# A two-layer decoder trunk on one core: two blocks of the expert product U h taken ahead of the second norm

## The chip, the core and the metric

The kernel runs on one core of one Trainium2 chip. The metric is the device time of one execution in microseconds (us). Five engines work from queues of their own and wait for one another through semaphores: TensorE (PE, matrix products), VectorE (DVE), ScalarE (ACT), GpSimd (POOL) and SyncE (SP, which here only issues transfers). ACT issues transfers too, from the same queue in which its arithmetic stands.

## The reference, cut to what matters (condensed)

A trunk of two layers on 512 tokens of width 1024. Each layer has a mixer (a gated MLP and stick-breaking attention, then an output projection) and an expert layer with 128 x 128 = 16384 single-neuron experts, of which each token takes 16 in each of 8 heads.

```python
for l in range(DEPTH):
    ...
    x = x + gt1 * jnp.einsum("btc,cd->btd", y_mix, w_out[l])
    h2 = rms_norm(x, norm2_g[l]) * (1.0 + sc2) + sh2
    x = x + gt2 * peer_layer(h2, peer_wq[l], peer_k1[l], peer_k2[l], peer_u[l], peer_v[l])

def peer_layer(h, w_q, k1, k2, u_tab, v_tab):
    q = h w_q                      # 8 heads of 128
    s1, s2 = q1 k1, q2 k2          # 128 scores each
    top 16 of s1, of s2, then of their 256 sums -> expert numbers, softmax g
    y = sum over the chosen experts of g * gelu(u_tab[e] . h) * v_tab[e]
```

`rms_norm` multiplies each token by the root r = 1/sqrt(mean(x^2) + eps), so h2 = r * (x * scale) + shift with scale = norm2_g * (1 + sc2) and shift = sh2, both one number per channel.

## The kernel before, in words

Everything is kept transposed: channels on the 128 partitions in 8 chunks (`xT`, 8 x 512), tokens along the free side. Products are taken in two halves: each operand is split into a rounded part and its remainder (`whi`, `wlo` for weights, `hhi`, `hlo` for h), and `mm3` (lines 331 to 336) does three matmuls for each chunk. A class `Stream` loads the weights in a written-out list (`entries`, lines 1021 to 1049) through a ring of raw tiles and prepares each tile ahead of its use: `whi` on ACT (line 91), `wlo` on DVE (line 92), into three slots.

The order of the instructions on each engine is set when the program is built, by a scheduler that goes by the order of the code, by priorities and by its own plan of the time. Each engine then runs its list in that order.

The places that matter here, for each layer:

- **Output projection** (`mixer`, lines 607 to 620). Eight blocks of 24 matmuls (`pout`), one for each chunk d of x. `out_block` adds the block to `xT` on DVE (line 608) and calls `Rms.step`, which squares the chunk on ACT (line 307) and sums the squares over the partitions with a matmul against ones (`ssq`, line 313; chunks 0 to 5 in pairs, 6 and 7 alone). After the last chunk `rsqrt` makes the root `rstd`: Ln and Exp on ACT (line 172) and four steps on DVE (lines 162 to 165), each in two parts.
- **Second norm** (`modulated`, lines 320 to 329). For each chunk `hpre` = x * scale * rstd on DVE, `hhi` = hpre + shift on ACT, `hlo` on DVE.
- **Routing, first half** (`route_phase`, lines 675 to 718). Per head the q projection (`pq`, 24 matmuls of 512 columns), scores against the keys `kb` (`sc`), and the two rounds of top 8 on DVE (`max`, `max_index`, `match_replace`, five lines, 704 to 708). Between the heads stand `WITH[h]` blocks of U h: `prefill` takes the product of 128 experts' rows of U with the first TD = 384 tokens (24 matmuls `pA`), applies gelu on ACT and stores the block to memory (`sp`) from ACT's queue. 60 of the 128 blocks are made in this way (`PRE`) during routing, the rest later.
- **Routing, second half** (lines 730 to 869). On DVE the candidates and the expert numbers (`route`), then tables of gates: `build` makes one-hot tiles on DVE (`o`, `gh`, `gl`), multiplies them on PE (`pg`), and ACT evicts (`sg`) and stores them, 2 MB at a time (`gd`). The remaining prefills are interleaved.
- **Dense phase** (`dense_phase`). For each of the 128 blocks: U h (read back from `sp`, or made now, `pA2`, four blocks ahead), times the gate (`gar`, which needs the loaded table `gt`), split, and multiplied with the rows of V into `yp` (18 matmuls). The last 128 tokens are done apart, with gathered rows on DVE.

Of the kernel before, what the change touches and what calls it, by code (L numbers as in the profile page):

```python
# [9 lines left out]
F32 = mybir.dt.float32  # L10
F32R = mybir.dt.float32r
# [4 lines left out]
AF = mybir.ActivationFunctionType  # L16
ALU = mybir.AluOpType
# [4 lines left out]
P = 128  # L22
L = 2
NC = 8
T = 512
# [3 lines left out]
PRE = 60  # L29
# [4 lines left out]

WITH = [0, 1, 1, 1, 1, 2, 1, 2]
SDELAY = 4.0
# [12 lines left out]
TD = 384  # L49
# [92 lines left out]
def tile_trunk(ctx, tc, a, dbg=None):  # L142
    nc = tc.nc
    V, S, G, PE = nc.vector, nc.scalar, nc.gpsimd, nc.tensor
# [43 lines left out]
    dram = ctx.enter_context(tc.tile_pool(name="dram", bufs=1, space=DRAM))  # L188
# [31 lines left out]
    xT = keep.tile([P, NC, T], F32, name="xT")  # L220
# [117 lines left out]

    def mixer(l, ws):
        with ExitStack() as st:  # L340
            mx = st.enter_context(tc.tile_pool(name="mx", bufs=1))
            tmp = st.enter_context(tc.tile_pool(name="mxt", bufs=2))
            pj = st.enter_context(tc.tile_pool(name="pj", bufs=2, space=PSUM))
            pn = st.enter_context(tc.tile_pool(name="pn", bufs=1, space=PSUM))
# [23 lines left out]

            va = mx.tile([P, 4, T], F32, name="va")
            vb = mx.tile([P, 4, T], F32, name="vb")  # L370
            uT = mx.tile([P, 4, T], F32, name="uT")
            qT, kT = [None] * 4, [None] * 4
            yb = mx.tile([P, 4, T], F32, name="yb")
            y = [uT[:, c, :] for c in range(4)] + [yb[:, c, :] for c in range(4)]
# [216 lines left out]
            for k in range(N + LAG2 + LAG3):  # L591
                if k < N:
                    s1(k)
                if 0 <= k - LAG2 < N:
                    s2(k - LAG2)
                if 0 <= k - LAG2 - LAG3 < N:
                    s3(k - LAG2 - LAG3)
                for x in PLAN[k].split():
                    if x[0] in "gns":
                        {"g": gmlp, "n": group_rms, "s": split_y}[x[0]](int(x[1]))  # L600
                        continue
                    name, n = x.split(":") if ":" in x else (x[0], x[1:])
                    for _ in range(int(n)):
                        next(steps[name])
            rms = Rms(tmp, py, "y")

            def out_block(d, ps):
                V.scalar_tensor_tensor(xT[:, d, :], ps, mod[l][:, 16 + d : 17 + d], xT[:, d, :], ALU.mult, ALU.add)
                rms.step(d)

            for _, w, ps in head:
# [4 lines left out]
            for d in range(2, NC):  # L616
                w, ps = wget(), pn.tile([P, T], F32, tag="n", name="pout") if d % 3 == 2 else pj.tile([P, T], F32, tag="pj", name="pout")
                for c in range(NC):
                    mm3(ps, w, c, c, c == 0, c == 7)
                out_block(d, ps)  # L620
            assert not ws.beside and not ws.behind
            ws.raw, ws.da, ws.spare = deque(RING_W + RING_A), RAW1 - 1, None
# [12 lines left out]

    def peer(l, ws, part):
        gd = dram.tile([NK // 4, P, TD // 32, P], F32, name=f"gd{l}")
        sp = dram.tile([PRE, P, TD], F32, name=f"sp{l}")
        with ExitStack() as outer:
# [11 lines left out]
    def route_phase(l, ws, st, gd, sp, hs, eid, gs):  # L651
# [7 lines left out]

            prefilled = [0]  # L660

# [359 lines left out]
    for l in range(L):  # L1021
# [13 lines left out]
        heads = [("w", a["w_all"][l, 28 + h]) for h in range(H)]  # L1035
        entries += heads[:2]
        for h in range(H):
# [12 lines left out]
        ws.beside = deque(rest)  # L1050
        mixer(l, ws)
        peer(l, ws, part)

# [58 lines left out]
```

## Time and profile before

| | |
|---|---|
| three runs, us | 2954.76, 2955.76, 2956.55; median 2955.76 |
| profiled execution, us | 2950.11, of which the profile's span holds 2948.4 |
| PE busy | 2845.9 us, 97% of the span |
| DVE busy | 2434.1 us, 83% |
| ACT busy | 1241.8 us, 42% |
| mean granted clock of PE | 0.985 of full speed |
| moved by DMA | 781.57 MB, 265 GB/s |

The times below are those of the profiled execution, in us from the start of its span. Layer 0 runs until about 1482, layer 1 after it. "Idle before" in a row, in square brackets, is the time for which the engine did nothing just before the instruction, with what ended it. The duration of a matmul in a row is longer than its place in the pipeline: the distance of two starts tells the pace.

### The profile page before, as it was taken

How to read it: one execution, taken by the hardware profiler on the slowest of the kernel's cores; microseconds unless marked ns; L12 is line 12 of the kernel's file. 1: busy time of each engine (PE TensorE's matmuls, PEld its weight loads, DVE VectorE, ACT ScalarE, POOL GpSimd, SP SyncE). 2: the span in 40 equal slices, each digit the busy share in tenths (PEclk: the TensorE clock that was granted, in tenths of full speed). 3: DMA queues.
4: the chain of work that ended last, by engine and by line, in shares of the span. 5: the costliest groups of instructions: out<-in, count | busy, mean ns of one | idle time of the engine just before them, and what ended most of it. 6: DMA issues, size and time to landing. Idle time of an engine off the chain costs nothing. (4 is left out here: it accounts for less than half of the span.)

```text
span 2948.4 us, 42181 instructions
## 1 busy us (share of the span) xinstructions
PE 2845.9 (97%) x15258; PEld 2468.4 (84%) x15258; DVE 2434.1 (83%) x4528; ACT 1241.8 (42%) x1736; POOL 724.9 (25%) x676
## 2 busy tenths in 40 slices
PE   7988999999999999999999899999999999999998
PEld 5755899988888888888877578999888888888886
DVE  7894999986888888888886759999688878888888
ACT  3553445554333333333354633555433333333332
POOL 1110000002443344343501000000044434444433
PEclk9998999999999999999999999999999999999999
DMA  8651245899999999999866023568899999999995
GB/s 289 221 187 58 85 153 177 258 266 363 352 330 350 331 335 360 332 349 335 289 206 207 22 73 118 167 210 265 274 393 329 353 330 350 335 338 347 335 352 181
DMA packets 317585, 781.57 MB, mean 265 GB/s; under 512 B 24912, under 2 KB 153968, under 8 KB 317376
## 3 DMA queue, kind: packets, MB, share of 16 engines
q1 hardware_dynamic: 116784, 398.51, 38.4%
q0 software_dynamic: 84048, 305.38, 28.5%
q10 hardware_dynamic: 116544, 74.98, 8.5%
q8 instruction: 119, 1.95, 0.3%
q14 instruction: 90, 0.74, 0.1%
HBM read 702.76 MB, written 76.02 MB: 264 GB/s over the span
## 5 line engine op out<-in xcount | busy, mean ns | idle before, releaser
L334 PE MATMUL pA<-hhi,whi 128*128 128x384 f32 x2048 | 692.5, 338 | 4.0 <-ACT whi L91 3.7
L336 PE MATMUL pA<-hhi,wlo 128*128 128x384 f32 x2048 | 691.4, 338 | 2.9 <-DVE wlo L92 2.7
L335 PE MATMUL pA<-hlo,whi 128*128 128x384 f32 x2048 | 690.8, 337 | 0.0
L898 POOL DMA_INDIRECT rows<-in_u,eid x256 | 335.0, 1309 | 1013.9 <-ACT whi L91 547.3
L91 ACT ACTIVATE whi<-raw 128x1024 fp32r<-128x1024 f32 x329 | 346.4, 1056 | 457.5 <-PE pA L335 268.1
L92 DVE TENSOR_TENSOR wlo<-raw,whi 128x1024 fp32r<-128x1024 f32 x329 | 400.2, 1218 | 131.3 <-ACT whi L91 124.9
L980 PE MATMUL yp<-vhi,wlo 128*128 128x512 f32 x1536 | 474.4, 390 | 0.0
L980 PE MATMUL yp<-vlo,whi 128*128 128x512 f32 x1536 | 474.3, 390 | 0.0
L980 PE MATMUL yp<-vhi,whi 128*128 128x512 f32 x1536 | 473.5, 390 | 0.0
L898 POOL DMA_INDIRECT rows<-in_v,eid x256 | 331.2, 1294 | 437.7 <-DVE junk L907 347.8
L334 PEld LDWEIGHTS pA<-hhi,whi 128*128 128x128 f32 x2048 | 385.7, 188 | 14.0 <-ACT whi L91 5.0
L335 PEld LDWEIGHTS pA<-hlo,whi 128*128 128x128 f32 x2048 | 385.6, 188 | 5.8
L336 PEld LDWEIGHTS pA<-hhi,wlo 128*128 128x128 f32 x2048 | 385.2, 188 | 5.7 <-DVE wlo L92 5.1
L969 ACT ACTIVATE whi<-gar 128x384 fp32r<-128x384 f32 x256 | 133.8, 523 | 544.3 <-PE yp L980 416.2
L92 DVE TENSOR_TENSOR vlo<-raw,vhi 128x1024 fp32r<-128x1024 f32 x256 | 312.5, 1222 | 46.8 <-ACT vhi L91 39.8
L980 PEld LDWEIGHTS yp<-vlo,whi 128*128 128x128 f32 x1536 | 288.3, 188 | 62.2
L980 PEld LDWEIGHTS yp<-vhi,wlo 128*128 128x128 f32 x1536 | 288.2, 188 | 61.4
L980 PEld LDWEIGHTS yp<-vhi,whi 128*128 128x128 f32 x1536 | 286.5, 188 | 51.4
L914 DVE SCALAR_TENSOR_TENSOR ys<-rows,wsp,ys 128x1024 f32<-128x1024 f32 x254 | 324.9, 1279 | 0.6
L907 DVE SCALAR_TENSOR_TENSOR junk<-rows,hs 128x1024 bf16<-128x1024 f32 x256 | 311.8, 1218 | 6.6 <-DMA rows<-in_u,eid 6.3
L91 ACT ACTIVATE vhi<-raw 128x1024 fp32r<-128x1024 f32 x256 | 271.1, 1060 | 75.2 <-PE yp L980 72.4
L970 DVE TENSOR_TENSOR wlo<-gar,whi 128x384 fp32r<-128x384 f32 x256 | 141.9, 556 | 95.4 <-ACT whi L969 89.9
(247 smaller groups left out, 3530.2 us busy)
## 6 DMA issues: line engine op xcount, KB each, us to landing
raw<-in_ut SPq DMA_DIRECT2D x256, 512.0 KB
raw<-in_v SPq DMA_DIRECT2D x256, 512.0 KB
gd<-sg ACTq DMA_DIRECT2D x24, 2048.0 KB
gt<-gd SPq DMA_DIRECT2D x64, 768.0 KB
raw<-in_w_all SPq DMA_DIRECT2D x66, 512.0 KB
rawa<-in_ada_w POOLq DMA_DIRECT2D x62, 512.0 KB
sp<-ga ACTq DMA_DIRECT2D x120, 192.0 KB
gar<-sp SPq DMA_DIRECT2D x120, 192.0 KB
```

The costliest lines, as they stand in the source:

```text
L91: i = self.nc.scalar.activation(hi[:, :n], r, AF.Copy)
L92: j = self.nc.vector.tensor_sub(lo[:, :n], r, hi.bitcast(F32)[:, :n])
L334: PE.matmul(ps, w[0][:, sl], hhi[:, m, :n], start=first, stop=False)
L335: PE.matmul(ps, w[0][:, sl], hlo[:, m, :n], start=False, stop=False)
L336: PE.matmul(ps, w[1][:, sl], hhi[:, m, :n], start=False, stop=last)
L898: tails["dma"] = G.indirect_dma_start(out=r, out_offset=None, in_=table, in_offset=bass.IndirectOffsetOnAxis(ap=eid[:, k : k + 1], axis=0) ...
L907: tc.keep_in_program_order(V.scalar_tensor_tensor(junk, r, 1.0, hs, ALU.mult, ALU.mult, accum_out=dots[:, k : k + 1]))
L914: tc.keep_in_program_order(V.scalar_tensor_tensor(ys, r, wsp[:, k : k + 1], ys, ALU.mult, ALU.add))
L969: S.activation(whi, ga, AF.Copy)
L970: V.tensor_sub(wlo, ga, whi.bitcast(F32))
L980: PE.matmul(yp[tb][e], w[wq][:, tt], vt[vq][:, e * T : (e + 1) * T], start=(i == 0 and wq + vq == 0), stop=(i == NK - 1 and wq == 1))
```

## The change

Two of the 60 early blocks per layer (`EARLY = 2`) are computed in `mixer`, right behind the output projection and without waiting for the root: the matmuls run on x * scale, split as `xhi` and `xlo` chunk by chunk inside `out_block`, and two columns are added to the 384 tokens, which hold the shift. The product is then U (x scale) * rstd + U shift: DVE multiplies the 384 columns by rstd, copies the one column of U shift, ACT applies gelu with that column as bias, and ACT's queue stores the block. The memory for `xhi` and `xlo` is that of `va`, `vb`, `uT` and `yb`, which are put into a pool of their own (`mv`) that is closed before. The two blocks stand at the front of the weight list, ahead of the q projection's first two tiles; the block that stood behind head 1 (`WITH`) is gone, and 50 instead of 51 are left for the second half of routing.

```diff
-WITH = [0, 1, 1, 1, 1, 2, 1, 2]
+WITH = [0, 0, 1, 1, 1, 2, 1, 2]
+
+EARLY = 2
...
+            act_st.close()
+            xs = st.enter_context(tc.tile_pool(name="xs", bufs=1))
+            xhi, xlo = ([xs.tile([P, 4, T], F32R, name=f"x{n}{i}") for i in range(2)] for n in ("hi", "lo"))
             rms = Rms(tmp, py, "y")
 
             def out_block(d, ps):
                 V.scalar_tensor_tensor(xT[:, d, :], ps, mod[l][:, 16 + d : 17 + d], xT[:, d, :], ALU.mult, ALU.add)
                 rms.step(d)
+
+                h, j = d // 4, d % 4
+                if j == 0:
+                    sh = mod[l][:, 24 + d : 28 + d].unsqueeze(2).to_broadcast([P, 4, 2])
+                    S.activation(xhi[h][:, :, TD : TD + 2], sh, AF.Copy)
+                    V.tensor_sub(xlo[h][:, :, TD : TD + 2], sh, xhi[h].bitcast(F32)[:, :, TD : TD + 2])
+                sc = svec[l][:, 1, d : d + 1]
+                S.activation(xhi[h][:, j, :TD], xT[:, d, :TD], AF.Identity, scale=sc)
+                V.scalar_tensor_tensor(xlo[h][:, j, :TD], xT[:, d, :TD], sc, xhi[h].bitcast(F32)[:, j, :TD], ALU.mult, ALU.subtract)
...
+            early = [(ws.get(), q.tile([P, T], F32, tag=x, name="pe")) for q, x in ((pj, "pj"), (pn, "n"))]
+            for c in range(NC):
+                for w, ps in early:
+                    sl, o = slice(c * P, (c + 1) * P), ps[:, : TD + 2]
+                    hi, lo = (t[c // 4][:, c % 4, : TD + 2] for t in (xhi, xlo))
+                    PE.matmul(o, w[0][:, sl], hi, start=(c == 0), stop=False)
+                    PE.matmul(o, w[0][:, sl], lo, start=False, stop=False)
+                    PE.matmul(o, w[1][:, sl], hi, start=False, stop=(c == NC - 1))
+            for b, (_, ps) in enumerate(early):
+                ga = tmp.tile([P, T], F32, tag="gr", name="gae")
+                V.tensor_mul(ga[:, :TD], ps[:, :TD], rstd[:, :TD])
+                V.tensor_copy(ga[:, TD : TD + 1], ps[:, TD : TD + 1])
+                S.activation(ga[:, :TD], ga[:, :TD], AF.Gelu_apprx_tanh, bias=ga[:, TD : TD + 1])
+                nc.scalar.dma_start(sp[b], ga[:, :TD])
...
-            prefilled = [0]
+            prefilled = [EARLY]
...
-        entries += heads[:2]
+        entries += ut[:EARLY] + heads[:2]
+        del ut[:EARLY]
```

The rest of the diff passes the store `sp` to both functions. Line numbers of the changed file are 2 higher up to line 339 and 26 higher in `route_phase` and `dense_phase`.

Three places show how the instructions moved. The order of layer 1 is the same at the first two. First PE in layer 0, at the end of the output projection: `ssq` is the sum of squares, `pe` an early block; this is the order of the changed program.

```order
L338 MATMUL pout<-hhi,wlo 128x512
L315 MATMUL ssq<-sq,ones 128x512
L639 MATMUL pe<-xhi_1743,whi 128x386
L640 MATMUL pe<-xlo_1745,whi 128x386
L641 MATMUL pe<-xhi_1743,wlo 128x386
```

23 matmuls of `pe` follow that `ssq` (the rows repeat), then the last `ssq`, that of chunk 7, then the other 25, then the q projection; before, the last `ssq` followed the other directly and the q projection came behind it.

Second, ACT in layer 0, from the root to the first `hhi`, with the semaphores that an instruction waits for. Before:

```order
L172 ACTIVATE rstd<-ssq,eps 128x256 [waits PE_49]
L172 ACTIVATE rstd<-ssq,eps 128x256
L172 ACTIVATE rstd<-rstd 128x256 [waits Activation_49] x2
L326 ACTIVATE hhi<-hpre,mod_120 128x512 [waits DMASW4_49,DMASW3_49,DVE_49]
L326 ACTIVATE hhi<-hpre,mod_120 128x512 [waits DVE_49] x7
```

And in the changed program:

```order
L174 ACTIVATE rstd<-rstd 128x256 [waits Activation_49] x2
L93 ACTIVATE whi<-raw 128x1024 [waits DMAHW1_49,PE_49]
L93 ACTIVATE whi<-raw 128x1024 [waits DMAHW2_49,PE_49]
L646 ACT_TABLE_LOAD
L646 ACTIVATE gae<-gae 128x384 [waits DVE_49] x2
L647 DMA sp_128<-gae 128x384 [waits Activation_49] x2
L328 ACTIVATE hhi<-hpre,mod_120 128x512 [waits DMAHW6_49,DMAHW4_49,DVE_49]
```

Two weight preparations, a table load, both gelus and both stores now stand between the root and the first `hhi`; the table load stood behind the first prefill of the routing before.

Third, DVE at the same place of the changed program:

```order
L167 SCALAR_TENSOR_TENSOR rstd<-sq,rstd 128x256 [waits DVE_49] x2
L644 TENSOR_TENSOR gae<-pe,rstd 128x384 [waits DVE_49,PE_49]
L645 COPY gae<-pe 128x1
L644 TENSOR_TENSOR gae<-pe,rstd 128x384 [waits PE_49]
L645 COPY gae<-pe 128x1
L94 TENSOR_TENSOR wlo<-raw,whi 128x1024 [waits DMAHW1_49,Activation_49]
L94 TENSOR_TENSOR wlo<-raw,whi 128x1024 [waits DMAHW2_49,Activation_49]
L326 SCALAR_TENSOR_TENSOR hpre<-xT,svec_122,rstd 128x512 [waits DMAHW6_49,DMAHW4_49,Activation_49]
```

Before, the first `hpre` followed the second `rstd` directly. `DMAHW4` and `DMAHW6` are the semaphores that the two stores of `gae` to `sp` raise, and the counts that `hpre`, `hhi` and the load of `kb` wait for are those after these stores. Counted over the rest of layer 0: from the first top-k step to the last `gl` DVE has 65 `wlo` before and 64 now; ahead of the first `pg` PE has 32.62 blocks of `pA` before and 31.62 now (besides the early two), from the first to the last `pg` 28.3 blocks of U h before and 28.4 now, and ahead of the first `yp` 65.33 before and 66 now with the early ones. Behind the last `gl`, the memset of `rows` stands ahead of two `wlo` before and behind them now.

## Rows read from the trace of the kernel before

**Rows 1.** The page: the span, and busy time of PE with its share and instructions.
```profile
span 2948.4 us, 42181 instructions
PE 2845.9 (97%) x15258; PEld 2468.4 (84%) x15258; DVE 2434.1 (83%) x4528; ACT 1241.8 (42%) x1736; POOL 724.9 (25%) x676
```
**Rows 2.** Windows, layer 0: length, PE, PEld, DVE, ACT, POOL busy, granted clock, DMA.
```profile
246.00:289.50 43.50, 41.67 (x160) 30.92 (x160) 21.21 (x25) 13.91 (x19) 1.07 (x2) 0.95 0.27 86
...
310.00:405.00 95.00, 94.98 (x575) 86.25 (x576) 94.56 (x528) 37.57 (x55) 0.00 (x0) 1.00 0.37 116
...
493.00:671.00 178.00, 171.57 (x1461) 161.02 (x1461) 157.81 (x162) 99.66 (x163) 0.00 (x0) 0.99 0.83 253
```
**Rows 3.** Windows around the second norm, layers 0 and 1.
```profile
289.50:294.70 5.20, 0.00 (x0) 0.00 (x0) 4.28 (x11) 2.11 (x6) 0.00 (x0) 0.69 0.37 102
294.70:298.40 3.70, 3.41 (x8) 2.61 (x9) 3.70 (x6) 1.97 (x3) 0.00 (x0) 0.52 0.00 0
...
1736.70:1742.00 5.30, 0.02 (x1) 0.02 (x1) 4.34 (x11) 2.22 (x6) 0.00 (x0) 0.69 0.33 99
```
**Rows 4.** Timeline, layer 0, around the second norm: start, length, engine, line, operation.
```profile
286.60 1.02 PE L313 MATMUL ssq<-sq,ones 128*128 128x512 f32 x2
...
288.27 1.12 PE L313 MATMUL ssq<-sq,ones 128*128 128x512 f32 x2 [0.65 <-ACT sq L307]
...
289.43 0.84 ACT L172 ACTIVATE rstd<-ssq,eps 128x256 f32<-128x256 f32 x2 [1.22 <-PE ssq L313]
...
292.31 0.75 DVE L165 SCALAR_TENSOR_TENSOR rstd<-sq,rstd 128x256 f32<-128x256 f32 x2
293.18 2.74 DVE L324 SCALAR_TENSOR_TENSOR hpre<-xT,svec,rstd 128x512 f32<-128x512 f32 x4
...
294.74 1.22 PE L334 MATMUL pq<-hhi,whi 128*128 128x512 f32 x2 [5.35 <-ACT hhi L326]
```
**Rows 5.** Timeline of PE, layer 0, inside a block of U h.
```profile
338.10 0.33 PE L334 MATMUL pA<-hhi,whi 128*128 128x384 f32 x1
...
338.62 0.33 PE L334 MATMUL pA<-hhi,whi 128*128 128x384 f32 x1
```
**Rows 6.** Timeline of ACT, layer 0, at the first prefill of the routing.
```profile
318.50 1.06 ACT L91 ACTIVATE whi<-raw 128x1024 fp32r<-128x1024 f32 x1 [3.11 <-PE pA L335]
319.58 1.28 ACT L672 ACT_TABLE_LOAD   x1
320.87 0.49 ACT L672 ACTIVATE ga<-pA 128x384 f32<-128x384 f32 x1
321.39 0.34 ACTq L673 DMA_DIRECT2D sp<-ga  x1
```
**Rows 7.** Durations of DVE lines 92, 970 and 800: ns least/median/most, first and last start.
```profile
L92 DVE TENSOR_TENSOR wlo<-raw,whi x329: 951/1221/1927, 24.8 to 2881.3; 128x1024 fp32r<-128x1024 f32 x165
...
L970 DVE TENSOR_TENSOR wlo<-gar,whi x256: 544/558/559, 690.3 to 2913.6; 128x384 fp32r<-128x384 f32 x128
...
L800 DVE RECIPROCAL sm<-sm x8: 175/190/197, 420.2 to 1948.5; 128x8 f32<-128x8 f32 x8
```
**Rows 8.** Chain that ended last, layer 1, end of routing: start, length, step.
```profile
2110.89 2.41 DMA sp<-ga
...
2116.57 14.30 DMA gd<-sg
```
**Rows 9.** Timelines of DVE and PE, layer 0, from routing to the dense phase.
```profile
684.22 0.06 DVE L897 MEMSET rows<- 128x1 f32 x1 [9.65 <-DMA gd<-sg]
...
688.43 1.96 DVE L966 TENSOR_TENSOR gar<-gar,gt 128x384 f32<-128x384 f32 x4 [1.13 <-DMA gt<-gd]
...
691.25 0.63 PE L980 MATMUL yp<-vhi,whi 128*128 128x512 f32 x2
```
**Rows 10.** Chain that ended last, layer 1, dense phase.
```profile
2161.77 4.12 PE yp L980 x18
```
**Rows 11.** Timeline, end of the program: the last four stores from ACT's queue.
```profile
2941.22 4.31 ACTq L1056 DMA_DIRECT2D out_y<-xT  x4
```

More of the change, by code (lines that the diff above doesn't have):

```diff
@@ L336, in mm3, with mixer @@
         PE.matmul(ps, w[1][:, sl], hhi[:, m, :n], start=False, stop=last)
-    def mixer(l, ws):
+    def mixer(l, ws, sp):
         with ExitStack() as st:
@@ L342, in mixer @@
             tmp = st.enter_context(tc.tile_pool(name="mxt", bufs=2))
+            act_st = st.enter_context(ExitStack())
+            mv = act_st.enter_context(tc.tile_pool(name="mv", bufs=1))
             pj = st.enter_context(tc.tile_pool(name="pj", bufs=2, space=PSUM))
@@ L367, in mixer @@
             nc.gpsimd.dma_start(bT, a["sgu_b"][l])
-            va = mx.tile([P, 4, T], F32, name="va")
-            vb = mx.tile([P, 4, T], F32, name="vb")
-            uT = mx.tile([P, 4, T], F32, name="uT")
+            va, vb, uT, yb = (mv.tile([P, 4, T], F32, name=n) for n in ("va", "vb", "uT", "yb"))
             qT, kT = [None] * 4, [None] * 4
-            yb = mx.tile([P, 4, T], F32, name="yb")
             y = [uT[:, c, :] for c in range(4)] + [yb[:, c, :] for c in range(4)]
@@ L634, in tile_trunk, with peer @@
         ORDER += range(4 * g, 4 * g + 4)
-    def peer(l, ws, part):
+    def peer(l, ws, part, sp):
         gd = dram.tile([NK // 4, P, TD // 32, P], F32, name=f"gd{l}")
-        sp = dram.tile([PRE, P, TD], F32, name=f"sp{l}")
         with ExitStack() as outer:
@@ L1050, in tile_trunk @@
         ws.beside = deque(rest)
-        mixer(l, ws)
-        peer(l, ws, part)
+        sp = dram.tile([PRE, P, TD], F32, name=f"sp{l}")
+        mixer(l, ws, sp)
+        peer(l, ws, part, sp)
     for c in range(NC):
```

## The prediction

> **What bounds the kernel now.** I read the page first for the engines: the tensor engine PE is busy 97% of a span of 2948.4 us [rows 1]. An average hides stages, so I next cut layer 0 into stages. While the output projection ends the mixer (246 to 289.5 us) PE is busy 41.7 of 43.5 us, the vector engine DVE 21.2 and the scalar engine ACT 13.9. In the top-k stage (310 to 405) PE and DVE are both full: 94.98 and 94.56 of 95 us. While the gate tables are built (493 to 671) DVE falls to 158 of 178 and PE stays at 172 [rows 2]. So from 310 us on nobody has room; what arrives late at the top-k stays late. Ahead of it lies the one hole. Around the second norm PE does nothing for 5.2 us, its granted clock falls to 0.69 of full, and the q projection after it begins at 0.52, that is near the lower level of 1.2 GHz, for 3.7 us; layer 1 shows the same hole [rows 3]. The hole is a chain: the last square matmul at 288.27, two ACT steps from 289.43, four pairs of DVE steps until 293.06, hpre at 293.18, first q matmul at 294.74 [rows 4]. The change puts two blocks of U h into that hole.
>
> What a block weighs: matmuls of 384 columns start 0.174 us apart (three between 338.10 and 338.62) [rows 5], so 24 take 4.2 us and two blocks 8.3.
>
> **The early work and what it displaces.** ACT gets eight xhi activations and DVE eight xlo steps per layer, about 0.5 and 0.56 us each by the rows of the same width [rows 6, 7]. They stand between steps of the output projection, which PE bounds and in which DVE was busy for less than half of the time and ACT for a third [rows 2]: nothing for them, and 8.5 us if that cover were gone.
>
> The order on PE costs something. The last square matmul now stands behind 23 early matmuls. PE ends the projection at 286.6, does the square of chunk 6 (about 0.9 us), and runs the 23 until 287.5 + 23 x 0.174 = 291.5, where the last square stood at 288.27: the norm is 3.2 us later, rstd ready at 296.3. The other 25 early matmuls end at 292.4 + 25 x 0.174 = 296.7.
>
> Then three engines must finish the early blocks ahead of hpre. On DVE: two products with rstd (0.56), two one-column copies (0.19 at most by the reciprocal of 8 columns) [rows 7], from 296.4 to 297.9; two wlo of 1.22, which waited for nothing here before, to 300.3. On ACT: the next two weight preparations, which wait for the slots of the early weights, 296.2 + 2 x 1.06 = 298.3; table load 1.28, 299.6; two gelus of 0.49, 300.6; the two stores are issued in 0.34 each, the second from 300.9 [rows 6].
>
> In the changed program hpre waits for the semaphores that the two stores raise on landing, and hhi and the kb load wait with it: hpre takes memory that the mixer's pools give back, and gae is among it. The row nearest to this price is the same kind of store on the chain of layer 1, 2.41 us from issue to landing [rows 8]; the last stores of the program, 256 KB each, bound it above: they are issued until 2945.53 and the span ends at 2948.4, so 2.9 us after the issue and 3.2 with it [rows 1, 11]. Below, it can be no less than its 0.34 of issue. I take 2.41, the same store. So hpre starts at 303.3 instead of 293.18: **10.1 us later**, and q with it. PE idles from 296.7 to 304.9, longer than the 5.2 us after which it restarted at 0.52, so the slow restart is paid as before and not saved.
>
> The table load deserves a sentence of its own. The row shows 1.28 us, begun as the preparation before it ends, with the gelu starting at 320.87, right behind it [rows 6]. The Trainium skill (ScalarE: Activation LUTs, What ACT_TABLE_LOAD costs) adds a drain of about 1.38 us to each switch. By that rule each layer would lose 1.4 us more and the forecast would rise by 2.8; this case's trace shows no such gap, and the sum goes by the row.
>
> **What it gives back.** Counted in the order of the instructions, DVE has 64 instead of 65 wlo between the first top-k step and the last gate step: -1.2 us in the full stages. On PE the same stretches lose one block, -4.2, but PE waits for DVE there (gates and weight halves), so the smaller number counts; the end of routing comes 8.9 later. Between first and last gate matmul PE has 28.4 blocks instead of 28.3: nothing.
>
> At the end of routing PE has done all it may when the last gate table is stored: that store takes 14.30 us [rows 8], and in layer 0 the memset that waits for it stands at 684.22, the first gates multiply at 688.43 after their load, and the first y matmul follows at 691.25 [rows 9]. In the change two wlo stand ahead of that memset, so PE runs on while the store lands: 66 instead of 65.33 blocks are done at the first y matmul. That start itself hangs on the store and the load, and moves only with the routing. From there on the dense phase is a chain of PE alone (18 y matmuls in 4.12 us, then the next block) [rows 10]: 0.67 blocks less, -2.8.
>
> **Sum per layer**: 10.1 - 1.2 - 2.8 = +6.1 us; two layers +12.2. The profiled execution took 2950.11, so 2962.3; the runs' median is 2955.76, 5.65 above, so in their terms 2955.76 + 12.2 = **2968.0**.
>
> Bounds: if PE alone decided until the last gate, 10.1 - 4.2 - 2.8 = +3.1 per layer, +6.2 in all, 2962. If the stores take 3.2 (+0.8), the order of blocks adds its 0.1 block (+0.5), and the y matmuls restart slowly after the longer wait in layer 0 (+1.8, half of the 3.7 us above), +9.2 per layer, 2974.
>
> **Rivals.**
>
> *The hole is filled and the chain hardly moves: faster.* For it: all operands of the first 24 early matmuls are there when the projection ends, and PE was idle. If the norm were held back by S, the balance per layer is S - 1.2 - 2.8, so it turns at S = 4.0 us; with S = 0 it is -4.0, or -7.0 if PE alone decides: 2942 to 2948. Against it: 3.2 us are lost by the place of the last square alone, and the early blocks' endings stand ahead of hpre on both engines. The Trainium skill (TensorE: Matmul & The Clock Gate, What's actually happening) speaks for this rival: the throttled clock is the default and activity releases it, so work in the hole would spare the q projection its slow start. By that rule 1.8 us more per layer would be saved, 2938 to 2944 in all; it holds only if no idle stretch is left between the early blocks and q, and before the change the clock was lost in 5.2 us of idling [rows 3].
>
> *The stores do not hold hpre, or DVE makes up the lag: no change.* Without them hpre stands behind the second wlo at 300.3, S = 7.1. If besides PE alone decides, 7.1 - 4.2 - 2.8 = +0.1 per layer: 2956. For it: DVE has 20 us free in the table building [rows 2]. Against it: there it waits for gates that PE makes in a fixed order.
>
> *The change's order is not what it says* (the early blocks running after the norm): the program rules this out; they stand ahead of the q projection.
>
> **How the numbers follow.** A difference under 0.2% (5.9 us) is about what a measurement of this kernel cannot tell from none. Forecast 0.66 (2962 to 2974, slower throughout); no change 0.21 (2950 to 2962), of which 0.01 lies above the line; faster 0.12; something larger than 2975, 0.01. Faster by over 0.2%: 0.12; within: 0.20; slower: 0.68. The forecast's own range is 2961 to 2975; to leave out no more than 2 in 10 the range goes down to 2955, into the case of no change.
>
> **What would show it.** In the profile after: the last ssq matmul behind 23 pe matmuls, some 3 us later relative to the projection; an idle stretch of about 8 us before the first q matmul, put down to hhi or hpre and these to the store of sp; a top-k stage that starts 10 us later after the projection's end and is as full as before; a dense phase that is a little shorter. The forecast is wrong if hpre starts less than 4 us late, if the stores land in much less than 2 us, or if the end of routing comes less than 4 us late although the top-k started 10 late.

## The result and the profile after

The changed kernel takes **2971.52 us** (median of 4 runs, 2971.04 to 2974.49) against 2955.26 us for the kernel before (4 runs, 2954.36 to 2956.55): ratio 1.0058, 95% interval 1.0046 to 1.0070, that is 17.1 us (13.6 to 20.7) slower by the ratio. The forecast was 2968.0, its range 2955 to 2975.

The two profiled executions lie further apart than the medians, 2948.4 and 2969.4 us of span. Some of that has nothing to do with the change: from the end of layer 0 to the end of layer 1's projection 255.4 us pass before and 257.6 after, in a stretch whose instructions are the same but for the eight `xhi` and `xlo` steps; in the experiments below it took 255.1 to 261.2, and 257.6 and 257.0 in the two kernels without those steps. So from here on each layer is measured from its own landmark, the square matmul of chunk 6 that closes the projection (286.60 before, 287.20 after in layer 0).

The page of the changed kernel, span and engines ([rows 1] before):

```profile
span 2969.4 us, 42230 instructions
PE 2849.8 (96%) x15258; PEld 2473.7 (83%) x15258; DVE 2445.7 (82%) x4556; ACT 1250.9 (42%) x1756; POOL 717.4 (24%) x676
```

PE is busy for 4 us more than before in a span that is 21 us longer: most of the loss is idling. To see where, I cut layer 0 at five landmarks: the projection's end, the first top-k step, the first and the last gate matmul, the first y matmul, the first transpose at the layer's end. Windows of the kernel before (length, then busy PE, PEld, DVE, ACT, POOL, granted clock, DMA share, GB/s):

```profile
286.60:312.40 25.80, 19.28 (x96) 14.77 (x95) 17.88 (x28) 12.50 (x21) 0.00 (x0) 0.87 0.11 26
312.40:493.18 180.78, 179.58 (x1051) 169.78 (x1050) 179.87 (x923) 84.75 (x109) 5.12 (x32) 1.00 0.46 143
493.18:670.38 177.20, 170.77 (x1456) 160.38 (x1456) 157.26 (x162) 98.86 (x161) 0.00 (x0) 0.99 0.83 254
670.38:691.25 20.87, 19.01 (x108) 18.36 (x107) 8.06 (x12) 7.77 (x13) 1.92 (x1) 1.00 0.90 305
691.25:1478.43 787.18, 787.18 (x3810) 694.63 (x3810) 651.56 (x832) 280.28 (x383) 332.53 (x260) 1.00 0.93 341
```

The same five of the changed kernel:

```profile
287.20:327.78 40.58, 29.56 (x153) 25.21 (x152) 21.82 (x35) 18.20 (x28) 1.06 (x2) 0.83 0.18 59
327.78:507.39 179.61, 176.43 (x1018) 165.71 (x1016) 178.70 (x922) 81.22 (x105) 5.13 (x32) 0.99 0.44 138
507.39:685.08 177.69, 170.23 (x1458) 159.42 (x1457) 158.38 (x163) 99.63 (x161) 0.00 (x0) 1.00 0.84 253
685.08:704.39 19.31, 18.09 (x98) 18.09 (x97) 4.81 (x8) 5.71 (x11) 1.02 (x1) 0.91 1.04 343
704.39:1488.73 784.34, 784.34 (x3794) 691.94 (x3794) 651.00 (x833) 280.65 (x384) 332.70 (x260) 1.00 0.92 338
```

The first stretch is 14.8 us longer (12.3 in layer 1); then 1.2 us come back up to the first gate matmul, the table building takes 0.5 us more, 1.6 come back ahead of the first y matmul and 2.8 in the dense phase. The later table has these five lengths for every kernel.

Inside the first stretch, the steps that answer to [rows 4]. Timeline of PE, ACT, DVE and POOL in layer 0 of the changed kernel (start, length, engine, line, operation, and the idle time before with what ended it):

```profile
292.08 1.02 PE L315 MATMUL ssq<-sq,ones 128*128 128x512 f32 x2
293.14 0.84 ACT L174 ACTIVATE rstd<-ssq,eps 128x256 f32<-128x256 f32 x2 [3.82 <-PE ssq L315]
296.03 0.75 DVE L167 SCALAR_TENSOR_TENSOR rstd<-sq,rstd 128x256 f32<-128x256 f32 x2
296.82 2.00 ACT L93 ACTIVATE whi<-raw 128x1024 fp32r<-128x1024 f32 x2 [2.22 <-PE pe L640]
298.07 2.35 DVE L94 TENSOR_TENSOR wlo<-raw,whi 128x1024 fp32r<-128x1024 f32 x2
298.84 1.28 ACT L646 ACT_TABLE_LOAD   x1
300.14 1.12 ACT L646 ACTIVATE gae<-gae 128x384 f32<-128x384 f32 x2
300.78 0.83 ACTq L647 DMA_DIRECT2D sp<-gae  x2
306.70 2.74 DVE L326 SCALAR_TENSOR_TENSOR hpre<-xT,svec,rstd 128x512 f32<-128x512 f32 x4 [6.28 <-DMA sp<-gae]
307.13 0.54 POOL L683 DMA_DIRECT2D kb<-in_k1T  x1 [95.78 <-DMA sp<-gae]
308.26 1.22 PE L336 MATMUL pq<-hhi,whi 128*128 128x512 f32 x2 [10.78 <-ACT hhi L328]
```

The chain that ended last, layer 1 of the changed kernel, shows the same place:

```profile
1759.30 1.13 ACT gae L646 x2
1760.45 5.11 DMA sp<-gae
1765.70 2.74 DVE hpre L326 x4
```

And the trace's summary for the stores in layer 0 (least, median, greatest of two):

```profile
DMA to landing us min/median/max: 5.3/5.4/5.5
```

This is the order of the releases: the root is there at 296.8, the second `wlo` at 300.4, the gelus at 301.3, and still `hpre` waits until 306.70 for the landing of the stores. Seen from the projection's end it starts 19.50 us later instead of 6.58, a lag of **12.9 us** (12.8 in layer 1). PE idles for 10.78 us.

### The profile page after: what moved, and what is told of

Read it like the earlier page. It is cut to its first block, busy times and chain, and to the rows that moved or that the text cites. A ratio compares the mean times of both kernels' runs of the same rounds, so it can differ in the third digit from the quotient of the medians.

```text
span 2969.4 us, 42230 instructions
## 1 busy us (share of the span) xinstructions
PE 2849.8 (96%) x15258; PEld 2473.7 (83%) x15258; DVE 2445.7 (82%) x4556; ACT 1250.9 (42%) x1756; POOL 717.4 (24%) x676
## 3 DMA queue, kind: packets, MB, share of 16 engines
q0 software_dynamic: 84048, 305.38, 28.5%
## 5 line engine op out<-in xcount | busy, mean ns | idle before, releaser
L338 PE MATMUL pA<-hhi,wlo 128*128 128x384 f32 x2016 | 682.6, 339 | 4.7 <-DVE wlo L94 4.6
L336 PE MATMUL pA<-hhi,whi 128*128 128x384 f32 x2016 | 682.8, 339 | 2.3 <-ACT gar L983 2.3
L337 PE MATMUL pA<-hlo,whi 128*128 128x384 f32 x2016 | 681.7, 338 | 0.0
L924 POOL DMA_INDIRECT rows<-in_u,eid x256 | 325.1, 1270 | 1041.3 <-DVE ys L940 356.8
L336 PEld LDWEIGHTS pA<-hhi,whi 128*128 128x128 f32 x2016 | 380.8, 189 | 10.8 <-issue 2.7
## 6 DMA issues: line engine op xcount, KB each, us to landing
gd<-sg ACTq DMA_DIRECT2D x24, 2048.0 KB, 11.2
```

The costliest lines, as they stand in the source:

```text
L336: PE.matmul(ps, w[0][:, sl], hhi[:, m, :n], start=first, stop=False)
L337: PE.matmul(ps, w[0][:, sl], hlo[:, m, :n], start=False, stop=False)
L338: PE.matmul(ps, w[1][:, sl], hhi[:, m, :n], start=False, stop=last)
L924: tails["dma"] = G.indirect_dma_start(out=r, out_offset=None, in_=table, in_offset=bass.IndirectOffsetOnAxis(ap=eid[:, k : k + 1], axis=0) ...
```

## Experiments

Theory A: what the change costs is the lag of the second norm, of which the landing of the two stores is the largest part; the full stages give back about 4 us a layer and no more. The rivals: the place of the last square (B), a lag that is made up later (C), and, once the first results were in, other causes for differences in the table building.

The table gives, for each kernel, the mean of both layers of its one profiled execution: **a** from the projection's end to the first top-k step, **b** to the first gate matmul, **c** to the last, **d** to the first y matmul, **e** to the first transpose, and in brackets PE's idle time in a and c. The last column is the ratio to the kernel before of the timed runs, with its interval. The stages end where an instruction starts in the timeline (c with the end of a matmul). A profiled execution can lie off its kernel's median, 5.65 us below it in the kernel before, 6.95 in e2 and 7.4 in e10; so the stages tell where time goes, and the ratio how much it is.

| kernel | a | b | c | d | e | sum | ratio |
|---|---|---|---|---|---|---|---|
| before | 26.3 (6.4) | 180.8 | 175.8 (5.7) | 21.6 | 787.3 | 1191.8 | 1 |
| changed | 39.8 (11.2) | 179.6 | 177.1 (7.0) | 19.8 | 784.4 | 1200.7 | 1.0058 (1.0046 to 1.0070) |
| e1 kept tile | 34.6 (5.1) | 180.0 | 173.0 (3.7) | 21.1 | 785.2 | 1193.9 | 1.0015 (1.0004 to 1.0025) |
| e2 square early | 40.1 (11.3) | 179.6 | 177.6 (7.3) | 20.5 | 784.4 | 1202.2 | 1.0074 (1.0058 to 1.0089) |
| e3 norm first | 33.8 (5.1) | 179.7 | 177.8 (7.3) | 20.1 | 784.4 | 1195.7 | 1.0014 (1.0006 to 1.0023) |
| e4 = e3 + square early | 29.1 (1.2) | 179.7 | 177.3 (7.0) | 20.8 | 784.4 | 1191.3 | 0.9988 (0.9976 to 0.9999) |
| e5 loads behind stores | 36.1 (7.0) | 179.6 | 177.1 (6.8) | 19.9 | 785.7 | 1198.5 | 1.0031 (1.0019 to 1.0042) |
| e6 block moved only | 27.0 (6.4) | 179.6 | 173.3 (3.5) | 19.5 | 792.8 | 1192.2 | 0.9994 (0.9984 to 1.0003) |
| e7 = e4, one block | 29.5 (5.0) | 179.7 | 175.6 (5.5) | 23.6 | 786.3 | 1194.7 | 1.0013 (1.0005 to 1.0022) |
| e8 = e4, gelus late, kept tile | 28.5 (0.7) | 180.1 | 173.0 (3.6) | 20.7 | 785.2 | 1187.4 | 0.9968 (0.9956 to 0.9980) |
| e12 = e4, kept tile | 29.2 (1.1) | 179.8 | 173.3 (3.7) | 20.6 | 785.2 | 1188.1 | 0.9977 (0.9966 to 0.9988) |
| e9 changed, stores on POOL | 39.7 (10.8) | 179.7 | 169.2 (0.8) | 20.7 | 785.2 | 1194.6 | 1.0002 (0.9991 to 1.0013) |
| e11 before, stores on POOL | 27.0 (6.4) | 180.8 | 167.8 (0.1) | 25.9 | 787.4 | 1188.9 | 0.9959 (0.9945 to 0.9973) |
| e10 = e8, stores on POOL | 28.5 (0.6) | 179.8 | 169.4 (0.7) | 20.5 | 785.2 | 1183.5 | 0.9949 (0.9936 to 0.9962) |

### e1: the stores no longer hold the norm

```diff
-                ga = tmp.tile([P, T], F32, tag="gr", name="gae")
+                ga = keep.tile([P, TD + 1], F32, tag="ga", name="gae", bufs=2)
...
-                ga = r1.tile([P, TD], F32, tag="ga", name="ga", bufs=GAB)
+                ga = (keep.tile([P, TD + 1], F32, tag="ga", name="ga", bufs=2) if b % 3 < 2 else r1.tile([P, TD + 1], F32, tag="ga", name="ga"))[:, :TD]
```

The second half is there because memory for two more tiles was not left: two of the three store tiles of the routing are now the same two.

> The changed kernel with one thing undone: the two tiles gae that the early stores read lie in memory that outlives the mixer, so hpre, hhi and the kb load no longer wait for the stores to land. Theory A (the landing of the two stores, 5.1 us after the second issue in layer 0, is the last wait in front of hpre): the first q matmul comes some 6 to 8 us earlier in each layer (302 instead of 308.26 in layer 0, relative to the end of the projection), and the time falls by about 12 to 14 us, from 2971.5 to 2958. Theory B (what holds the norm back is the last square behind 23 early matmuls, and the rest is in its shadow): no more than 2 us. Theory C (the top-k has slack after all, so the lag is made up later): q earlier, the time unchanged.

Measured 1.0015, 12.7 us less than the changed kernel's 1.0058. Timeline of PE, layer 0:

```profile
304.13 0.97 PE L336 MATMUL pq<-hhi,whi 128*128 128x512 f32 x2 [3.94 <-ACT hhi L328]
```

That is 14.2 us behind the projection's end (289.90) instead of 21.1, 6.8 earlier, as A has it; B falls, and C, since the time follows. But only 5.3 of the 6.9 us per layer lie in a, where the wait was. The table building is 4.1 shorter as well, and d 1.3 longer. The edit did a second thing, which e9 to e12 take up.

### e2: the last square earlier

```diff
+                    if k >= 3:
+                        after(i, tails["ssq"])
+                    k += 1
```

(`i` is the first matmul of each three of the early blocks, `tails["ssq"]` the last square.)

> The changed kernel with the last square matmul in front of the tenth early matmul instead of the twenty-fourth. Theory A (the early matmuls' end, then the products, gelus and stores, hold hpre; the root is ready just when they end and is not the last thing): the root is ready about 2.5 us earlier, but hpre starts where it did (306.7 in layer 0, within 0.7 us), and the time stays at 2971 within 3. Theory B (each us by which the norm is late is a us of the layer): hpre 2.5 us earlier in each layer, 2966.

Measured 1.0074, not below the changed kernel's 1.0058. That is 4.7 us above it by the ratios, more than the 3 that A allows, but the two intervals overlap. Timeline of PE, DVE and ACT, layer 0:

```profile
287.89 1.02 PE L315 MATMUL ssq<-sq,ones 128*128 128x512 f32 x2
291.83 0.75 DVE L167 SCALAR_TENSOR_TENSOR rstd<-sq,rstd 128x256 f32<-128x256 f32 x2
295.25 0.56 DVE L648 TENSOR_TENSOR gae<-pe,rstd 128x384 f32<-128x384 f32 x1 [2.67 <-PE pe L645]
305.22 2.74 DVE L326 SCALAR_TENSOR_TENSOR hpre<-xT,svec,rstd 128x512 f32<-128x512 f32 x4 [6.55 <-DMA sp<-gae]
```

The root is ready 2.5 us earlier (behind the projection's end), the product waits for PE, and `hpre` starts 19.76 us behind the projection instead of 19.50. The place of the square costs nothing as long as the ends of the early blocks stand ahead of `hpre`.

### e3 and e4: the norm ahead of the ends of the early blocks

e3 writes the norm's eight steps first and lets the early blocks accumulate in another PSUM buffer:

```diff
-            early = [(ws.get(), q.tile([P, T], F32, tag=x, name="pe")) for q, x in ((pj, "pj"), (pn, "n"))]
+            pe = pz.tile([P, 2, T], F32, tag="z", name="pe")
+            early = [(ws.get(), pe[:, b]) for b in range(EARLY)]
...
+            modulated(l, 1, tmp)
             for b, (_, ps) in enumerate(early):
...
-                modulated(l, 1, tmp)
                 first = [(ws.get(), psA.tile([P, T], F32, tag="A", name="pq")) for _ in range(2)]
```

> The changed kernel with the second norm's eight steps written ahead of the products, gelus and stores of the early blocks (which accumulate in another PSUM buffer so that q need not wait for them). The last square stays behind 23 early matmuls. Theory A: hpre follows the root directly (about 297 in layer 0 instead of 306.7), the first q matmul behind the two weight preparations at about 299.5 instead of 308.3, and hlo some 6 us earlier: the time falls by 12 to 17 us to 2955 to 2959. Theory B: the norm is as late as in the change, so that 3 to 4 us per layer stay and the time is 2962 or more.

e4 adds e2's edit and does the two blocks one behind the other:

```diff
-            for c in range(NC):
-                for w, ps in early:
+            for w, ps in early:
+                for c in range(NC):
```

> Both of the last two, and the two early blocks one behind the other instead of interleaved, so that the slot of the first one's weights is free earlier. Theory A: PE runs from the projection through 48 early matmuls into the q projection with less than 1 us of idling in between (q at about 297.3 in layer 0), at a granted clock near 1; what is left of the change is its gain, and the time falls below the kernel before: per layer q is 2 us later than before, the slow restart of q (1.8 us) is spared, 1.2 and 2.8 us come back later: about 2948 to 2952. The rival that filling the hole gives nothing, since DVE sets the end of the top-k: 2953 to 2957.

e3 measured 1.0014, that is 2959.4 us on the kernel before's 2955.26, just above A's range and below B's. `hpre` follows the root and starts 9.9 us earlier than in the change (9.6 against 19.5 behind the projection), but `hlo` stands behind two products and two `wlo` and comes 6.5 us earlier only; a falls by 6.0. In e4 almost nothing is left in the way. Timeline of PE, layer 0 (the last early matmul, the first of q, and the first wait in q):

```profile
294.94 0.34 PE L646 MATMUL pe<-xhi,wlo 128*128 128x386 f32 x1
295.11 0.63 PE L336 MATMUL pq<-hhi,whi 128*128 128x512 f32 x2
296.63 0.50 PE L337 MATMUL pq<-hlo,whi 128*128 128x512 f32 x1 [0.67 <-DVE hlo L329]
```

And its window from the first q matmul on:

```profile
295.11:298.80 3.69, 3.02 (x16) 2.44 (x16) 3.69 (x9) 3.67 (x5) 0.00 (x0) 1.00 0.28 105
```

In 3.7 us PE issues 16 matmuls at a granted clock of 1.00; before it were 8 at 0.52 [rows 3]. The ratio is 0.9988, the kernel before is beaten by 3.5 us (0.3 to 7.1), near the lower end of the 3 to 7 us that I expected. The lag in a is 2.8 us, and b to e give back 3.3.

### e5: what the landing depends on

```diff
+            ws.pa = 1
             early = [(ws.get(), q.tile([P, T], F32, tag=x, name="pe")) for q, x in ((pj, "pj"), (pn, "n"))]
...
-                nc.scalar.dma_start(sp[b], ga[:, :TD])
+                ws.late = nc.scalar.dma_start(sp[b], ga[:, :TD]).ins.name
+            ws.order, ws.lates, ws.pa = after, 3, 2
...
+        if self.lates:
+            self.lates -= 1
+            self.order(i, self.late)
```

(`i` is the `whi` of a preparation; SP issues a weight load when the tile of a prepared weight comes free.)

> The changed kernel with the two weight preparations on ACT ordered behind the two early stores instead of ahead of the gelus, so that the two weight loads of 512 KB which SP issued just ahead of the stores (299.31 and 300.44 against 300.78 in layer 0) start behind them. hpre still waits for the stores. Theory A (the stores took 5.4 and 5.1 us to land because they shared the DMA engines with these loads, not because a store costs this): issue to landing falls to 2.4 to 3.0 us, hpre starts some 5 us earlier (about 14 us behind the projection's end instead of 19.5), the first hlo some 4 us earlier, and the time falls by about 8 us against the changed kernel, to a ratio of about 1.003 to the kernel before. Theory B (two stores landing together in front of a waiting engine cost 5 us in any case): landing stays near 5 us, hpre 2.5 us earlier at most, ratio 1.005 or more.

In the changed kernel the loads went out just ahead of the stores, the second `sp<-gae` at 301.3:

```profile
299.31 0.33 SPq L80 DMA_DIRECT2D raw<-in_w_all  x1
300.44 0.33 SPq L80 DMA_DIRECT2D raw<-in_ut  x1
```

In e5 both stores go first; timeline and the landing of the stores, layer 0 (layer 1 has the same 1.9):

```profile
296.65 0.86 ACTq L652 DMA_DIRECT2D sp<-gae  x2
299.84 2.73 DVE L330 SCALAR_TENSOR_TENSOR hpre<-xT,svec,rstd 128x512 f32<-128x512 f32 x4
299.95 0.33 SPq L81 DMA_DIRECT2D raw<-in_w_all  x1
```
```profile
DMA to landing us min/median/max: 1.9/1.9/1.9
```

1.9 us instead of 5.1 to 5.5: a store of 192 KB is late because two loads of 512 KB were issued 0.3 and 1.5 us ahead of it. The early stores of the other kernels bear this out. In e7, e8 and e10, where the last load had been issued at least 5.3 us before and had landed, they took 1.9 us; in e9, with the change's two loads ahead, 4.9 to 5.4. One load is enough: in e12 a single one went out 0.02 us ahead of the first store of each layer, and the four stores took 4.8 to 5.7:

```profile
DMA to landing us min/median/max: 4.8/5.2/5.7
```

The Trainium skill (DMA: Bandwidth & Descriptors, Queues, rings and completion order) says that each DMA engine takes packets from the queues in turn, so that SP's loads and ACT's stores share the same engines; the two durations agree. `hpre` starts 5.2 us earlier behind the projection, and the ratio is 1.0031. Not all of the 5.2 is the landing: 3.4 us are. The edit also lets the table load run ahead of the root's end and the gelus ahead of the preparations, so that the second store goes out 2.5 us earlier; 0.7 us are lost to the `wlo` that now ends last ahead of `hpre`.

### e6: the moved block alone

One constant of the kernel before: `WITH` becomes `[0, 0, 1, 1, 1, 2, 1, 2]`, no early blocks.

> The kernel before with one constant of the change alone: the block of U h that stood behind head 1 moves to the later ones, and no early block is taken. It measures what the sum of the prediction gave back and what it would have cost without early blocks: DVE has 64 instead of 65 wlo from the first top-k step to the last gate step (1.2 us less), and PE has done 64 instead of 65.33 blocks when the first y matmul runs (5.6 us more of the dense phase). By these counts: first y matmul 1.2 us earlier or the same, dense phase 5.6 us longer, +4.4 us per layer, a ratio of 1.003. The rival (all blocks have to be made anyway, so moving one costs nothing): 1.000, within 0.001.

The counts came true and the sum did not. b falls by 1.2 and e rises by 5.6, as counted; but c and d shorten by 4.7 together, and the whole is 0.9994 (0.9984 to 1.0003), no change, as the rival has it. I had held the first y matmul to be fixed by DVE and by the last store. It comes 5.8 us earlier behind the first top-k step, about the weight of the 1.33 blocks (5.6) that PE has less to do before it. But PE's count does not fix it alone. The changed kernel makes the same 64 blocks between the projection and the first y matmul, besides the early two, and has the same b and the same 64 `wlo`; yet its c is 3.9 us longer, and PE idles there for 7.0 us instead of 3.5. PE's order of blocks and gate matmuls is another in the two kernels; why it waits less in e6 stays open. The moved block by itself costs and gives nothing that the interval shows, so the 4 us of the changed kernel are not due to this constant: measured from e6, the early blocks alone take 8.4 us out of e, of which c and d take 4.2 back.

### e7: one early block

`EARLY = 1` in e4.

> The kernel that puts the norm first and the last square early (0.9988 of the kernel before), with one early block instead of two. Theory A (the hole holds 5.3 us of PE, and one block of 4.2 us fits into it): q starts within 0.7 us of where it does in the kernel before, measured from the end of the projection, the first hlo is at most 0.7 us later, DVE has 64 instead of 65 wlo in the full stages (-1.2) and 65.54 instead of 65.33 blocks are done at the first y matmul (-0.9): 1.4 to 4 us less per layer, a ratio of 0.997 to 0.999. Rival (two blocks are better, since each later block is worth its 4.2 us): above 0.999.

Measured 1.0013: A falls, and the rival's range is met. Timeline of PE, layer 0, the waits inside q:

```profile
297.63 0.73 PE L336 MATMUL pq<-hhi,whi 128*128 128x512 f32 x2 [3.65 <-ACT hhi L328]
300.06 0.80 PE L337 MATMUL pq<-hlo,whi 128*128 128x512 f32 x1 [1.48 <-DVE hlo L329]
```

And two windows of q:

```profile
297.63:301.30 3.67, 2.19 (x7) 1.72 (x8) 3.67 (x8) 3.64 (x5) 0.00 (x0) 0.71 0.34 125
301.30:305.00 3.70, 3.70 (x12) 3.02 (x12) 3.70 (x7) 2.51 (x5) 0.00 (x0) 0.50 0.15 53
```

Behind one block PE idles for 3.65 and 1.48 us, and q runs at a granted clock of 0.71 and then 0.50, the lower level (in layer 1 at 0.50 from its start). So a is as long as with two blocks, 29.5 against 29.1, and the block that was not made in the hole comes later: c, d and e are 3.0 us longer together than in e4. The rival put a later block at 4.2 us; by the sums it is 3.4. Two blocks pay here also because they leave no idle stretch, and not only because they are two.

### e8 and e12: gelus behind the norm, and the kept tile by itself

e8 keeps the tiles as in e1 and orders products and gelus of the early blocks behind the last `hlo` (the gelus and stores written in `route_phase`, ahead of the loop over heads):

```diff
+                after(V.tensor_mul(ga[:, :TD], ps[:, :TD], rstd[:, :TD]), tails["hlo"])
...
+                for b, ga in enumerate(gaes):
+                    after(S.activation(ga[:, :TD], ga[:, :TD], AF.Gelu_apprx_tanh, bias=ga[:, TD : TD + 1]), tails["hlo"])
+                    nc.scalar.dma_start(sp[b], ga[:, :TD])
```

> The kernel that puts the norm first and the last square early, with the products, gelus and stores of the two early blocks ordered behind the last hlo and their tiles in memory that outlives the mixer. Theory A: the steps of the early blocks (1.4 us on DVE, 3.2 us on ACT) no longer stand between the norm's steps, PE's waits of 0.67 and 0.23 us inside the q projection go, and the first top-k step comes 0.5 to 1.5 us earlier: ratio 0.997 to 0.9985. Rival (PE with its 48 early matmuls, not the norm's steps, now sets the start and the pace of q): same as with the steps in between, 0.9985 to 0.9995.

e12 is e4 with e1's edit and nothing else.

> The kernel with the norm first and the last square early (0.9988), with the early tiles in memory that outlives the mixer and nothing else: it parts the two edits of the kernel with the gelus behind the norm (0.9968). Theory A (what that kernel gained lay in the gate stage, 177.3 to 173.0 us, where a store behind a gate table's issue held ACT for 4.8 us instead of 5.3 once two of the three store tiles lay elsewhere; not in the norm's steps, where the first top-k step came only 0.6 us earlier): gate stage about 173 us, ratio 0.997 to 0.998. Theory B (the order of the gelus did it): gate stage about 177 us, ratio 0.9985 to 0.9995.

0.9968 and 0.9977. Stage a gains 0.6 us in e8 and nothing in e12; the table building is 4.1 to 4.4 shorter in both. So by the sums 3.2 of e8's 3.9 us are the kept tile's, in a stage that the edit was not aimed at; what the order of the gelus adds, the intervals leave open.

### e9, e10, e11: the stores of the routing on GpSimd's queue

One line of `prefill` in the changed kernel (e9), in e8 (e10) and in the kernel before (e11):

```diff
-                nc.scalar.dma_start(sp[b], ga)
+                nc.gpsimd.dma_start(sp[b], ga)
```

> The changed kernel with the stores of the routing's blocks of U h issued by GpSimd's queue instead of ACT's (the two early stores stay on ACT). In the traces so far such a store that stands behind the issue of a 2 MB gate table holds ACT for 5 us, and PE waits for sg in the table building (7.5 us of idling in layer 0 of the changed kernel). Theory A (these holds set the gate stage's length, and the runs differ there by how the stores fall): the holds on ACT are gone, the stretch from the first to the last gate matmul falls from 177 to about 171 us in both layers, and the ratio from 1.006 to about 1.002. Theory B (the stage is bound by PE's and DVE's work, the holds are hidden): the stretch stays within 2 us, the ratio at 1.005 or more. The wait of hpre for the early stores is as in the changed kernel in both.

> The kernel with the norm first, the square early and gelus behind the norm (0.9968 of the kernel before) with the routing's stores on GpSimd's queue. Theory A: its gate stage (172.6 and 173.3 us) loses the 3.3 to 3.9 us that PE still idles there: ratio about 0.994 to 0.995. Theory B: as without it, 0.996 to 0.998.

> The kernel before with the routing's stores on GpSimd's queue, nothing else: the control that says whether the effect has to do with the early blocks. Theory A: the gate stage falls from 177.2 and 174.4 to about 171 us, ratio about 0.997. Theory B: 0.999 to 1.001.

All three go A's way, and c falls a little further than I expected (169.2 and 167.8 instead of 171 us). What PE waited for in the table building of the kernel before, layer 0 (us in total, times, longest; 6.4 us of idling in all), and the timeline of ACT there, with a store behind the issue of a 2 MB gate table:

```profile
PE pg L844 <- ACT sg L846: 6.2, 9, 2.4
```
```profile
641.96 0.38 ACTq L848 DMA_DIRECT2D gd<-sg  x1
642.37 5.43 ACTq L673 DMA_DIRECT2D sp<-ga  x1
648.19 1.58 ACT L846 ACTIVATE sg<-pg 128x512 f32<-128x512 f32 x3 [5.88 <-issue]
```

In layer 0 the first store behind each of the first eleven gate tables took 0.9 to 6.4 us to issue, and 5.3 to 5.4 in the four that follow the table's issue directly; all others took 0.33. The evictions `sg` stand behind it, and PE waits for them: 5.7 us of idling per layer in c, nearly all of it for `sg`. On GpSimd's queue a store takes 0.54 us, and PE is idle for 0.1 us in c of e11, 0.8 in e9. Windows of c in layer 0 of e11 and e9:

```profile
491.29:659.06 167.77, 167.64 (x1456) 158.27 (x1456) 155.21 (x160) 97.90 (x158) 15.18 (x28) 1.00 0.86 266
506.07:675.18 169.11, 168.38 (x1458) 158.61 (x1457) 158.23 (x163) 100.54 (x161) 14.57 (x27) 1.00 0.87 266
```

In d, 4.3 us are lost again in e11, and 0.9 in e9. In e11 the last gate table's store is issued 4.0 us behind the last gate matmul instead of 0.7, since a `vhi` ahead of it on ACT waits for a store of `sp` to land; the memset of `rows` waits for that table's store. Timeline of ACT and DVE, layer 0 of e11:

```profile
660.04 2.01 ACT L91 ACTIVATE vhi<-raw 128x1024 fp32r<-128x1024 f32 x2 [4.44 <-DMA sp<-ga]
663.05 0.37 ACTq L848 DMA_DIRECT2D gd<-sg  x1
676.48 0.06 DVE L897 MEMSET rows<- 128x1 f32 x1 [9.93 <-DMA gd<-sg]
```

In the kernels with the kept tile (e1, e8, e12) the last three of these long issues in layer 0 took 4.7 to 4.9 us, in the changed kernel, e3, e4 and e5 5.2 to 5.5, with the same order of instructions on ACT in the table building in e4 and e8; why the tile's place matters there stays open.

e10 is the fastest kernel of the study, 2941.94 us, 0.9949 of the kernel before. But e11 reaches 0.9959 without any early block: what the early blocks add on top is not settled by these intervals.

## Why the prediction was right

The sign, the place and the mechanism of the loss came as forecast, and 2971.5 lies inside both ranges. Of what comes back, the number came nearer than its reasons. By its steps:

- **The last square 3.2 us later**: 4.88 us behind chunk 6's square instead of 1.67, so 3.2. **Early matmuls until 296.7**: until 297.5, with a projection that ended 0.6 later.
- **DVE and ACT ahead of `hpre`**: second `wlo` done at 300.4 (300.3), gelus at 301.3 (300.6), second store issued at 301.3 (300.9). The table load took 1.28 us, begun at 298.84, and the gelu started at 300.14: no gap for a drain. By the rule of the Trainium skill (ScalarE: Activation LUTs, What ACT_TABLE_LOAD costs), which adds one, it would have come 1.4 us later; the trace disagrees here.
- **The stores' landing, 2.41 us, upper bound 3.2**: this is the term that was mis-sized. It measured 5.1 to 5.5, above the bound. The row that I took was the same kind of store, but I did not ask what else would be in flight: the two `wlo` that I had put ahead of `hpre` myself free two load tiles, and SP issues two loads of 512 KB into the stores. e5 shows it. Nor did the program's last stores bound such a store: the routing's own, of the same size, landed in 1.8 to 12.2 us in the changed kernel. The lag is 12.9 instead of 10.1.
- **PE idle from 296.7 to 304.9 and the slow restart not saved**: 10.78 us, then 0.50 in q. In e4, with 48 early matmuls and no break, q ran at 1.00. The rule of the Trainium skill (TensorE: Matmul & The Clock Gate, What's actually happening), that the slow clock is the default and activity lifts it, agrees with both; it did not come to bear in the change.
- **-1.2 in the full stages, -2.8 in the dense phase**: b is 1.2 shorter, e 2.8 and 2.9. Not in the sum were c (+0.5 and +2.2) and d (-1.6 and -2.2). That these nearly cancel, so that b to e gave back 4.6 us where 4.0 were foretold, is luck.
- **Why it comes back** was only half right. I let DVE's count decide until the last gate. In b it does: with 64 `wlo` b is 179.6 in the changed kernel and in e6, although PE idles there longer than before (2.7 and 3.2 us instead of 1.4). In c it does not: e11 shows that PE's waits in the table building came from ACT's queue, not from DVE. And the first y matmul moves with neither count alone (e6).
- **Sum**: +6.1 a layer foretold, +9.0 by the stages and +8.6 by the ratio: 2.8 us more of lag at `hpre`, 0.7 more until the first top-k step, and 0.6 more given back. The forecast of 2968.0 is 3.5 us short.

Of the rivals, "the hole is filled" was said to turn at a lag of 4.0 us. Stage a is longer than before by 13.6, 13.8, 9.9, 7.5 and 2.8 us in the changed kernel, e2, e5, e3 and e4, where the routing's stores were left as they were, and the sums differ by 9.0, 10.5, 6.7, 4.0 and -0.5: between 3.2 and 4.6 us less each time. So each us of lag is about a us of the layer, and the turning point lies near where it was put. "No change", with stores that do not hold `hpre`, is what e1 tried: 1.0015, but with 4.1 us a layer less in the table building, which goes with the tiles' place. The lag there was not the 7.1 of that rival: `hpre` starts 3.8 us later than in the kernel before, the first q matmul 6.1 and the first top-k step 8.3.

## What to carry to other kernels

Work that is put into a hole of one engine brings its endings along: ask where its evictions, table loads and stores stand in the other engines' queues, and order them behind the chain that the hole was waiting for (e4, e8). Memory that is given back while a store still reads it turns the store's landing into a wait of the next pool's first user, and that landing is to be priced with the loads that will be in flight then, not with a lone store's. In this kernel a block that was only moved from one full stage to another was worth nothing that could be measured (e6); what counted was idle time that was filled (e4) and a wait that was removed (e5, e11).

## What the runs showed that I had not expected

- A store of 192 KB landed in 1.9 us with no load in flight (e5, e7, e8, e10), in 5.1 to 5.5 with two loads of 512 KB issued 0.3 and 1.5 us ahead of it, and in 4.8 to 5.7 with one issued 0.02 us ahead (e12).
- The issue of a small store on ACT's queue took 5.3 to 5.4 us right behind the issue of a 2 MB store on the same queue, and 0.33 where none was near. Moving the small stores to GpSimd's queue (0.54 us each) took 0.41% (0.27 to 0.55) off the kernel before; the filled hole alone (e4) took 0.12% (0.01 to 0.24).
- PE's granted clock was 1.00 in q after 10.1 us without a break, and 0.71, then 0.50 after waits of 3.65 and 1.48 us (e4, e7, layer 0).
